# Weight sums', sample and state transfers issued by GpSimd, the second tokens' first gates in 256, 256 and 512 columns, and another place for the gates' buffers

## The chip, the cores and the metric

One core of a Trainium2 chip runs the kernel. The metric is the device time of one execution in microseconds; the time before is the median of three runs. A profile of one execution stands beside it. Its engines are called PE (TensorE), DVE (VectorE), ACT (ScalarE), POOL (GpSimd) and SP (SyncE, which only issues transfers here). SPq, ACTq and POOLq are the queues in which SP, ACT and POOL issue DMAs, each in its own order.

## The reference

One layer of a hybrid decoder: 2048 prompt tokens of width 1024 in one batch, and 8 sample sequences of one token each with states of their own.

```python
ada = silu(c) @ w_ada + b_ada
shift, scale, gate = split(ada, 3)
hn = rmsnorm(x, g_norm) * (1 + scale) + shift
z = hn @ w_in                                  # 1024 -> 5136
xa, za, q, k, v, glr, zg = split(z, ...)       # 1024, 1024, 512, 512, 1024, 16, 1024

xc = conv_b + sum(xp[:, j:j + T] * conv_w[j] for j in range(4))
gx = sigmoid(blocks(xc) @ w_gate_x + b_gate_x)     # 8 blocks of 128
ga = sigmoid(blocks(xc) @ w_gate_a + b_gate_a)
a = exp(8 * ga * log_sigmoid(lru_lambda))
u = sqrt(1 - a * a) * gx * xc
h_t = a_t * h_{t-1} + u_t
y_lru = h * silu(za)

log_alpha = log_sigmoid(glr @ w_gla_g2 + b_gla_g2) / 16
S_t = diag(alpha_t) S_{t-1} + k_t^T v_t ; o_t = q_t S_t     # 4 heads, 128 x 256 states
y_gla = rmsnorm(o) * g_gla_norm * silu(zg)

x = x + gate * (concat(y_lru, y_gla) @ w_out)
y = rmsnorm(x, g_final)
```

The outputs are y for prompt and samples and the new states (recurrence, convolution, GLA).

## The kernel before

All products are made in split form: an operand is cut into a high part (`hh`, `hi`) and a low part (`hl`, `lo`), and each product is three matmuls, high by high, high by low and low by high. Lines 650 to 652 (`project`) make tiles of w_in's columns by tokens, with 24 matmuls for a tile; lines 335 to 337 (`value_mm`) make the GLA values; line 1515 (`product`) and line 1801 (`Pair.product`) make seven products in place of eight, from sums and differences of blocks (Strassen's scheme).

The work goes through the prompt in two halves of 1024 tokens (`TH`). In the first half, for each of the four GLA heads in the order 3, 0, 1, 2, `gla_head` makes values, keys, queries and gates and runs chunks of 128 tokens, and `lru` makes some of the eight recurrence tiles. The weights used in both halves are split once and stored in DRAM as `parts`; `weights` loads them again in the second half (line 302: `w<-parts`) into one of three buffers with tag `w`.

Between the halves, `lru_last_a` normalizes and modulates the second tokens (`modulate`: PE transposes, ACT scales, POOL writes `hh` at line 201, DVE writes `hl` at line 202). These steps lie in a list, `drips`, of which `project` runs one after every second block of 128 rows. Then come `gates_ahead` (the gates of head 3, by `project`), and `gates_seven` and `lru_seven` for the three other heads and two recurrence tiles, with seven products. ACT stores the gates to DRAM (`zgd`, lines 1576 and 1603), and `gate_load` (line 1174) brings them back when a head of the second half needs them. In the second half `gla_head(1, h)` and `lru` alternate; the last stage, from line 1645, multiplies by w_out, with seven products for each pair of token tiles, from sums of w_out's blocks (`wd`, `wd2`).

Those sums are made beside the other work. `pair_weights` loads a pair of w_in's column tiles (`tr`, line 749), makes four differences with DVE, splits them and stores them (`twd`, line 763), five pairs in all. When it is done, `out_weights` starts: 16 steps, each of which loads a part of w_out (`r`, line 810), multiplies it by the gate, makes the sums (line 828), in half of the steps splits two of them (lines 832 and 833), and stores seven or nine pieces (lines 837 and 846). It stops ahead of the second tokens' preparation and goes on in the second half.

The order of this side work is written by a clock of units: `after(units, f)` puts a function off, and `tick` moves the clock on, by one unit for each projected tile and by half a unit for each value tile, and runs what is due. `behind(V)` queues what it encloses behind the last DVE instruction. `tc.tile_pool` gives buffers by tag; a buffer of a tag, or a pool opened where another was closed, waits for the last use of what lay there. A list scheduler with costs of its own puts independent instructions into each engine's order; within an engine they run in that order, so that what stands behind a waiting instruction waits too.

The pool `sp`, opened by `open_sp`, holds the buffers of the second tokens' preparation in six places of equal size with tags s0 to s5, in order of allocation: `fs4` (s0, s1, s2), `xst` (s3, s4, s5), and later over them the operands of the seven products and, at tag s2, `zq`, the buffers of the last gates. `close_sp` closes it and opens the pools of the second half's heads, whose values `vh` and `vl` are the first to be written.

Of the kernel before, what the change touches and what calls it, by code (L numbers as in the profile page):

```python
# [54 lines left out]
def hybrid_kernel(ctx, tc, i, o):  # L55
# [588 lines left out]
    def project(w, c0, n, mid=None):  # L644
# [3 lines left out]
        for kt in range(KT):  # L648
# [6 lines left out]
            if kt % 2:  # L655
                drip()
# [84 lines left out]
    def pair_weights(n=0):  # L741
# [6 lines left out]
        for a, col in enumerate(cols[n]):  # L748
            SP.dma_start(r[:, a], i["w_in"][0, :, col:col + P].rearrange("(k p) n -> p k n", p=P))
# [5 lines left out]
        def split(k, x):  # L755
            def f():
# [3 lines left out]

                def store():
                    for u, y in enumerate((t.bitcast(F32), x)):
                        SP.dma_start(twd[n, k, :, u], y.rearrange("p k n -> p (k n)"))

                after(0.5, store)
            return f

        def one(ops):
            if not ops:
                pair_weights(n + 1)  # L770
                return
            with behind(V):
                for f in ops[0]:
                    f()
            after(0.5, lambda: one(ops[1:]))

        halves = [split(k, x) for k, x in enumerate((b11, b22, b12, b21))]
        after(1.5, lambda: one([[sub(b11, b12, b11), sub(b12, b22, b12)], [sub(b22, b22, b11), sub(b21, b21, b22)],
                                halves[:2], halves[2:]]))

    def out_weights(s0=0):


        def begin(s):
# [5 lines left out]
            SP.dma_start(g, dram(gated, (8 + 32 * q) * 256, [[0, P], [64 * 256, 2], [1, 256]]))  # L790
            SP.dma_start(bt, dram(i["b_ada"], 2 * D + q * 256, [[0, P], [512, 2], [1, 256]]))
# [13 lines left out]
        def load(s):  # L805
            q, f, m = where(s)
            r = hp.tile([P, 2, 2, 256], F32, tag="r", name="r")
            for a in range(2):
                k = CTS[f] + 4 * a + m
                SP.dma_start(r[:, a], i["w_out"][0, k * P:(k + 1) * P].rearrange("p (b n) -> p b n", b=2)[:, :, q * 256:q * 256 + 256])  # L810
            return r

        def one(ops, end):
# [5 lines left out]
            after(0.5, (lambda: one(ops[1:], end)) if ops[1:] else end)  # L819

        def step(s, r, g):
# [8 lines left out]
            def split(n, x):  # L830
# [3 lines left out]

                def store2():
                    for h in range(2):
                        SP.dma_start(wd2[n, :, h, m, c], p[:, h].bitcast(F32))

                after(0.5, store2)

            def store():

                for x, ops in ((r[:, 0], (B11, T1)), (r[:, 1], (B21, B22)), (t, (T2, T3, T4))):
                    for n, k in enumerate(ops):
                        if not (f and k in (B22, T4)):
                            SP.dma_start(wd[f, k, :, m, c], x[:, n])
                if outw["stop"] or s == 15:
                    outw["busy"], outw["next"] = False, s + 1
                elif s % 8 < 7:
                    after(0.5, lambda: again(s + 1, g))  # L850
                elif q == 0:
                    after(0.5, lambda: begin(s + 1))
# [4 lines left out]
                + ([[lambda: split(0, b22), lambda: split(1, t[:, 2])]] if f else []), lambda: after(0.5, store))  # L857

        def again(s, g):
            r = load(s)  # L860
            after(1.5, lambda: step(s, r, g))
# [1352 lines left out]
```

## Time and profile before

| | us |
|---|---|
| median of 3 runs | 1481.87 |
| lowest and highest | 1480.29, 1484.11 |
| the profiled execution | 1483.09 |
| its span | 1481.3 |
| PE busy | 1432.7 |
| DVE busy | 1050.7 |
| ACT busy | 691.2 |
| POOL busy | 30.0 |

The span is the time from the first to the last instruction in the profile. Busy time of PE is not PE at its peak: matmuls overlap, and a matmul after idle time can run at a lower clock. In the lists of waits, a row names the waiting engine, tile and line, then what it waited for, then total, number and longest. In a timeline a row has the start, the duration, the engine, the line, the operation with its tiles, and in brackets the idle time before it and what ended it.

### The profile page before, as it was taken

To read this page: it belongs to the slowest core of one execution; us is meant where nothing else is said; L and a number is where in the kernel's file an instruction comes from. 1 tells how busy PE (TensorE), PEld (TensorE's weight loads), DVE (VectorE), ACT (ScalarE), POOL (GpSimd) and SP (SyncE) were. 2 spreads that over 40 slices of the span, in tenths; PEclk is the share of its full clock that TensorE was granted. 3 is DMA by queue.
4 is the path that set the end of the run, shared out by engine and by line. 5 is a ranking of instruction groups with operands and counts; after the bars stand their busy time and mean duration, and the time that the engine had idled before them with its cause. 6 is when DMAs were issued, how large, how long until landed. Compare 5 with 4: busy or idle time off the path is not lost.

```text
span 1481.3 us, 23382 instructions
## 1 busy us (share of the span) xinstructions
PE 1432.7 (97%) x8693; PEld 1253.9 (85%) x8693; DVE 1050.7 (71%) x2471; ACT 691.2 (47%) x1253; POOL 30.0 (2%) x44
## 2 busy tenths in 40 slices
PE   8999999999999999999899999798999999999998
PEld 6888989889898887787799999798998887778886
DVE  5757667765765868844458688487678886588886
ACT  4654544652554466633354444445457622244342
POOL 0200000000000002000000000000000000000000
PEclk9999999999999999999999999899999999999999
DMA  9656976856555554666836647467462757793453
GB/s 328 256 181 206 302 261 204 262 164 201 176 188 189 177 189 147 220 217 220 302 116 203 225 148 225 137 205 240 143 209 91 298 179 270 262 354 120 141 174 114
DMA packets 206135, 305.31 MB, mean 206 GB/s; under 512 B 13570, under 2 KB 143778, under 8 KB 203581
## 3 DMA queue, kind: packets, MB, share of 16 engines
q1 hardware_dynamic: 171317, 282.58, 56.9%
q10 hardware_dynamic: 34352, 20.19, 4.4%
q8 instruction: 68, 1.11, 0.3%
q0 software_dynamic: 352, 1.05, 0.2%
q14 instruction: 46, 0.38, 0.1%
HBM read 188.51 MB, written 115.33 MB: 205 GB/s over the span
## 4 chain that ended last, share of the span: by engine, by line
PE 77%; DVE 11%; DMA 6%; ACT 4%; issue 2%; SPq 0%; POOL 0%; ACTq 0%; DVEq 0%
PE acc L1801 12%; PE acc L650 10%; PE acc L651 10%; PE acc L652 10%; PE tp L1801 9%; PE acc L1515 5%; PE acc L335 3%; PE acc L336 3%; PE acc L337 3%; DMA w<-parts 3%; PE po L1045 1%; DVE cv L1239 1%; PE tp L1131 1%; DMA tr<-in_w_in_dram 1%; PE acc L1276 1%
## 5 line engine op out<-in xcount | busy, mean ns | idle before, releaser
L650 PE MATMUL acc<-hh,w 128*128 128x512 f32 (+3 forms) x1096 | 385.4, 352 | 14.4 <-DMA w<-parts 14.1
L651 PE MATMUL acc<-hl,w 128*128 128x512 f32 (+3 forms) x1096 | 374.4, 342 | 2.7 <-DVE hl L202 2.7
L652 PE MATMUL acc<-hh,w 128*128 128x512 f32 (+3 forms) x1096 | 373.9, 341 | 0.0
L650 PEld LDWEIGHTS acc<-hh,w 128*128 128x128 f32 x1096 | 207.6, 189 | 34.2 <-issue 10.0
L651 PEld LDWEIGHTS acc<-hl,w 128*128 128x128 f32 x1096 | 207.6, 189 | 20.9 <-DVE hl L202 4.2
L652 PEld LDWEIGHTS acc<-hh,w 128*128 128x128 f32 x1096 | 207.3, 189 | 17.0
L1801 PE MATMUL acc<-w,a 128*128 128x512 f32 (+1 forms) x792 | 184.8, 386 | 0.0
L1801 PEld LDWEIGHTS acc<-w,a 128*128 128x128 f32 x792 | 146.8, 188 | 33.2 <-issue 3.4
L335 PE MATMUL acc<-w,hh 128*128 128x256 f32 (+1 forms) x508 | 145.8, 287 | 2.4 <-DVE zq L1098 1.3
L337 PE MATMUL acc<-w,hl 128*128 128x256 f32 (+1 forms) x508 | 143.4, 282 | 0.0
L336 PE MATMUL acc<-w,hh 128*128 128x256 f32 (+1 forms) x508 | 143.3, 282 | 0.0
L1801 PE MATMUL tp<-w,a 128*128 128x512 f32 x564 | 136.0, 391 | 0.0
L1801 PEld LDWEIGHTS tp<-w,a 128*128 128x128 f32 x564 | 105.3, 188 | 26.8 <-issue 5.2
L335 PEld LDWEIGHTS acc<-w,hh 128*128 128x128 f32 x508 | 96.4, 190 | 5.2 <-DVE zq L1098 1.8
L337 PEld LDWEIGHTS acc<-w,hl 128*128 128x128 f32 x508 | 96.7, 190 | 0.0
L336 PEld LDWEIGHTS acc<-w,hh 128*128 128x128 f32 x508 | 96.4, 190 | 0.1
L1097 ACT ACTIVATE zs<-acc 128x512 f32<-128x512 f32 (+3 forms) x69 | 34.4, 498 | 104.9 <-PE acc L652 97.6
L1239 DVE SCALAR_TENSOR_TENSOR cv<-xa,vecT,cv 128x512 f32<-128x512 f32 (+2 forms) x120 | 76.1, 637 | 9.2 <-ACT cv L1237 8.7
L1651 ACT CAST a<-s 128x512 fp32r<-128x512 f32 x61 | 36.5, 619 | 95.7 <-issue 36.1
L1098 DVE SCALAR_TENSOR_TENSOR zs<-zs,acc 128x512 f32<-128x512 f32 (+3 forms) x69 | 38.7, 560 | 45.6 <-ACT zs L1097 45.6
L928 ACT CAST vh<-acc 128x256 fp32r<-128x256 f32 x56 | 20.7, 371 | 89.1 <-PE acc L337 71.1
L929 DVE TENSOR_TENSOR vl<-acc,vh 128x256 fp32r<-128x256 f32 x56 | 23.5, 420 | 51.5 <-ACT vh L928 51.4
(377 smaller groups left out, 2557.3 us busy)
## 6 DMA issues: line engine op xcount, KB each, us to landing
parts<-w SPq DMA_DIRECT2D x37, 1024.0 KB
w<-parts SPq DMA_DIRECT2D x28, 1024.0 KB
wr<-in_w_in_dram SPq DMA_DIRECT2D x44, 512.0 KB
a<-mixd SPq DMA_DIRECT2D x63, 256.0 KB
w<-wd SPq DMA_DIRECT2D x12, 1024.0 KB
w<-twd SPq DMA_DIRECT2D x20, 512.0 KB
mixd<-zs ACTq DMA_DIRECT2D x34, 256.0 KB
wada<-in_w_ada_dram SPq DMA_DIRECT2D x16, 512.0 KB
```

Of the source, the lines that this page charges most:

```text
L335: PE.matmul(ps, hh[:, kt, c], hi[:, kt % 4], start=kt == 0, stop=False)
L336: PE.matmul(ps, hh[:, kt, c], lo[:, kt % 4], start=False, stop=False)
L337: PE.matmul(ps, hl[:, kt, c], hi[:, kt % 4], start=False, stop=kt == KT - 1)
L650: PE.matmul(ps[:, :n], hi[:, kt], a, start=kt == 0, stop=False)
L651: PE.matmul(ps[:, :n], hi[:, kt], b, start=False, stop=False)
L652: PE.matmul(ps[:, :n], lo[:, kt], a, start=False, stop=kt == KT - 1)
L1097: S.activation(z, ps, AF.Tanh, scale=0.5)
L1098: V.scalar_tensor_tensor(z, z, 1.0, ps, op0=OP.add, op1=OP.mult)
L1239: V.scalar_tensor_tensor(cv[:, cq], xa[:, cq.start + k:cq.stop + k], cw[k], cv[:, cq], op0=OP.mult, op1=OP.add)
L1515: PE.matmul(ps, w[:, u, k], x[v][k], start=start and (k, u, v) == (0, 0, 0), stop=(k, u) == (3, 1), skip_group_check=True)
L1651: S.copy(t[:, 0, k], (low(t) if src is None else src)[:, k])
L1801: PE.matmul(ps, t[:, u, k], w[:, v, k, c], start=(q < 3 or ps is own) and (k, u, v) == (0, 0, 0), stop=(k, u) == (3, 1), skip_group_check= ...
```

## The change

Seven things are done.

- `project` runs a drip after every second block as before when the tile is wider than 256 columns, and after every fourth block when it is not.
- GpSimd issues what SP issued before: the loads and stores of `pair_weights` and of `out_weights`, the stores of the sample values (`vsd`), and the stores of the sample GLA states.
- In `pair_weights` and `out_weights` the stores follow directly on the operations, not half a unit later, and the next load follows directly on the stores. The first operation on a loaded tile is due two units after the load, not one and a half. In `pair_weights` each operation is queued behind DVE by itself.
- In the second half, `gate_load` is called with the first chunk's products, not with the chunk's start.
- `open_sp` allocates the place s2 last, behind s3 to s5.
- `gates_ahead` makes the gates of the second tokens in pieces of 256, 256 and 512 columns, not 512 and 512.
- With that, its remaining drips are run and the sums are begun after the second piece of 256.

```diff
@@ -652,7 +652,7 @@
             PE.matmul(ps[:, :n], lo[:, kt], a, start=False, stop=kt == KT - 1)
             if mid and kt == 3:
                 mid()
-            if kt % 2:
+            if kt % 2 and (n > 256 or kt % 4 == 3):
                 drip()
         return ps[:, :n]
 
@@ -746,7 +746,7 @@
             return
         r = hp.tile([P, 2, KT, P], F32, tag="tr", name="tr")
         for a, col in enumerate(cols[n]):
-            SP.dma_start(r[:, a], i["w_in"][0, :, col:col + P].rearrange("(k p) n -> p k n", p=P))
+            G.dma_start(r[:, a], i["w_in"][0, :, col:col + P].rearrange("(k p) n -> p k n", p=P))
         b11, b21, b12, b22 = r[:, 0, :4], r[:, 0, 4:], r[:, 1, :4], r[:, 1, 4:]
 
         def sub(x, y, z):
@@ -757,25 +757,21 @@
                 t = hp.tile([P, 4, P], F32R, tag="th", name="th", bufs=2)
                 S.copy(t, x)
                 V.tensor_tensor(x, x, t.bitcast(F32), op=OP.subtract)
-
-                def store():
-                    for u, y in enumerate((t.bitcast(F32), x)):
-                        SP.dma_start(twd[n, k, :, u], y.rearrange("p k n -> p (k n)"))
-
-                after(0.5, store)
+                for u, y in enumerate((t.bitcast(F32), x)):
+                    G.dma_start(twd[n, k, :, u], y.rearrange("p k n -> p (k n)"))
             return f
 
         def one(ops):
-            if not ops:
+            for f in ops[0]:
+                with behind(V):
+                    f()
+            if ops[1:]:
+                after(0.5, lambda: one(ops[1:]))
+            else:
                 pair_weights(n + 1)
-                return
-            with behind(V):
-                for f in ops[0]:
-                    f()
-            after(0.5, lambda: one(ops[1:]))
 
         halves = [split(k, x) for k, x in enumerate((b11, b22, b12, b21))]
-        after(1.5, lambda: one([[sub(b11, b12, b11), sub(b12, b22, b12)], [sub(b22, b22, b11), sub(b21, b21, b22)],
+        after(2, lambda: one([[sub(b11, b12, b11), sub(b12, b22, b12)], [sub(b22, b22, b11), sub(b21, b21, b22)],
                                 halves[:2], halves[2:]]))
 
     def out_weights(s0=0):
@@ -787,8 +783,8 @@
 
             g = hp.tile([P, 2, 256], F32, tag="g", name="g")
             bt = hp.tile([P, 2, 256], F32, tag="t", name="bt")
-            SP.dma_start(g, dram(gated, (8 + 32 * q) * 256, [[0, P], [64 * 256, 2], [1, 256]]))
-            SP.dma_start(bt, dram(i["b_ada"], 2 * D + q * 256, [[0, P], [512, 2], [1, 256]]))
+            G.dma_start(g, dram(gated, (8 + 32 * q) * 256, [[0, P], [64 * 256, 2], [1, 256]]))
+            G.dma_start(bt, dram(i["b_ada"], 2 * D + q * 256, [[0, P], [512, 2], [1, 256]]))
             r = load(s)
 
             def add():
@@ -807,7 +803,7 @@
             r = hp.tile([P, 2, 2, 256], F32, tag="r", name="r")
             for a in range(2):
                 k = CTS[f] + 4 * a + m
-                SP.dma_start(r[:, a], i["w_out"][0, k * P:(k + 1) * P].rearrange("p (b n) -> p b n", b=2)[:, :, q * 256:q * 256 + 256])
+                G.dma_start(r[:, a], i["w_out"][0, k * P:(k + 1) * P].rearrange("p (b n) -> p b n", b=2)[:, :, q * 256:q * 256 + 256])
             return r
 
         def one(ops, end):
@@ -816,7 +812,10 @@
             with behind(V):
                 for f in ops[0]:
                     f()
-            after(0.5, (lambda: one(ops[1:], end)) if ops[1:] else end)
+            if ops[1:]:
+                after(0.5, lambda: one(ops[1:], end))
+            else:
+                end()
 
         def step(s, r, g):
             t = hp.tile([P, 3, 256], F32, tag="t", name="t")
@@ -831,34 +830,30 @@
                 p = hp.tile([P, 2, 256], F32R, tag="p", name="p", bufs=2)
                 S.copy(p[:, 0], x)
                 V.tensor_tensor(p[:, 1], x, p[:, 0].bitcast(F32), op=OP.subtract)
-
-                def store2():
-                    for h in range(2):
-                        SP.dma_start(wd2[n, :, h, m, c], p[:, h].bitcast(F32))
-
-                after(0.5, store2)
+                for h in range(2):
+                    G.dma_start(wd2[n, :, h, m, c], p[:, h].bitcast(F32))
 
             def store():
 
                 for x, ops in ((r[:, 0], (B11, T1)), (r[:, 1], (B21, B22)), (t, (T2, T3, T4))):
                     for n, k in enumerate(ops):
                         if not (f and k in (B22, T4)):
-                            SP.dma_start(wd[f, k, :, m, c], x[:, n])
+                            G.dma_start(wd[f, k, :, m, c], x[:, n])
                 if outw["stop"] or s == 15:
                     outw["busy"], outw["next"] = False, s + 1
                 elif s % 8 < 7:
-                    after(0.5, lambda: again(s + 1, g))
+                    again(s + 1, g)
                 elif q == 0:
-                    after(0.5, lambda: begin(s + 1))
+                    begin(s + 1)
 
             one([[op(r[:, 0], r[:, 0], g, OP.mult), op(r[:, 1], r[:, 1], g, OP.mult)],
                  [op(t[:, 1], b22, b12, OP.subtract), op(b12, b12, b11, OP.subtract),
                   op(t[:, 0], b22, b12, OP.subtract), op(t[:, 2], b21, t[:, 0], OP.subtract)]]
-                + ([[lambda: split(0, b22), lambda: split(1, t[:, 2])]] if f else []), lambda: after(0.5, store))
+                + ([[lambda: split(0, b22), lambda: split(1, t[:, 2])]] if f else []), store)
 
         def again(s, g):
             r = load(s)
-            after(1.5, lambda: step(s, r, g))
+            after(2, lambda: step(s, r, g))
 
         begin(s0)
 
@@ -898,7 +893,7 @@
             (S.copy if g % 2 else V.tensor_copy)(vs[r, :min(n4, DV - g * n4)], ps[r, :min(n4, DV - g * n4)])
         for g in range(4):
             c = slice(g * n4, min((g + 1) * n4, DV))
-            SP.dma_start(vsd[h][:, c], vs[32 * g:32 * g + NS, :c.stop - c.start])
+            G.dma_start(vsd[h][:, c], vs[32 * g:32 * g + NS, :c.stop - c.start])
         if n > DV:
             r = slice(96, 96 + NS)
             return low_rank(ps[r, DV - 3 * n4:n4], r, TH)
@@ -1081,7 +1076,7 @@
         po = psum.tile([P, 512], F32, tag="o", name="po", bufs=1)[:, :DV]
         for n in (3, 0, 1, 2):
             PE.matmul(po[32 * n:32 * n + 32], qm[:, b0 + n], s0[:, n], start=True, stop=True)
-        SP.dma_start(o[7][0, b0:b0 + 4, h].rearrange("b k v -> k b v"), s0)
+        G.dma_start(o[7][0, b0:b0 + 4, h].rearrange("b k v -> k b v"), s0)
         if b0 == 0:
             V.tensor_copy(os_, po)
             return
@@ -1152,10 +1147,10 @@
             nch = min(SEGS[half][s][1], TH - SEGS[half][s][0]) // P
             if c == 0:
                 prep[s, "run"] = gla_start(half, h, s, prep[s])
-                if half:
-                    gate_load(s)
                 after(PACE[half][0], lambda: chunks(s, 1), True, True)
                 return
+            if c == 1 and half:
+                gate_load(s)
             gla_chunk(half, h, s, c - 1, prep[s], prep[s, "run"], v)
             if c < nch:
                 after(PACE[half][1], lambda: chunks(s, c + 1), True, True)
@@ -1165,7 +1160,7 @@
             if s + 1 < ns:
                 after(0, lambda: chunks(s + 1, 0), True, True)
             elif half == 1:
-                SP.dma_start(o[4][0, 0, h], St[h])
+                G.dma_start(o[4][0, 0, h], St[h])
 
         def gate_load(s):
             c0, n = SEGS[half][s]
@@ -1419,8 +1414,9 @@
         hpx.close()
         nonlocal sp_
         sp_ = spx.enter_context(tc.tile_pool(name="sp", bufs=1, side="right", reuse_waits="tile"))
-        fs4[:] = [sp_.tile([P, 4, 512], F32, tag=f"s{n}", name="fs4") for n in range(3)]
+        fs4[:] = [sp_.tile([P, 4, 512], F32, tag=f"s{n}", name="fs4") for n in range(2)]
         xst[:] = [sp_.tile([P, 2, D], F32, tag=f"s{n}", name="xst") for n in range(3, 6)]
+        fs4.append(sp_.tile([P, 4, 512], F32, tag="s2", name="fs4"))
         ra[:] = [new_ra(F32) for _ in range(2)]
 
     def new_ra(dt):
@@ -1597,12 +1593,12 @@
     def gates_ahead(h):
 
         w = [weights(ZG + (2 * h + dt) * P, P) for dt in range(2)]
-        for c0, n in SEGS[0]:
+        for c0, n in ((0, 256), (256, 256), (512, 512)):
             for dt in range(2):
                 z = silu2(w[dt], c0, n)
                 S.dma_start(zgd[2 * h + dt][:, c0:c0 + n], z)
-                tick()
-            if c0 == 0:
+                tick(n / 512)
+            if c0 == 256:
                 while drips:
                     drip()
                 sums()
```

## The prediction

> **What bounds the kernel now.** I began with the page: TensorE is busy 97% of the span, so a change gains only what TensorE's idle time holds, and the clock lost behind it.
>
> ```profile
> span 1481.3 us, 23382 instructions
> ...
> PE 1432.7 (97%) x8693; PEld 1253.9 (85%) x8693; DVE 1050.7 (71%) x2471; ACT 691.2 (47%) x1253; POOL 30.0 (2%) x44
> ```
>
> That leaves 1481.3 - 1432.7 = 48.6 us idle. The waits of TensorE (line, what was waited for: total us, times, longest) say which part of it this change can reach, and the waits of SP's queue say what SP stood behind.
>
> ```profile
> PE acc L650 <- DMA w<-parts: 14.1, 3, 8.0
> PE tp L878 <- DVE g L872: 3.0, 1, 3.0
> PE acc L651 <- DVE hl L202: 2.7, 2, 2.5
> ...
> SPq L846 <- DVE r L828: 80.7, 19, 20.2
> SPq L837 <- DVE p L833: 27.4, 6, 6.9
> ```
>
> Three kinds carry 19.8 us: stored weight parts that land late in the second half's heads (14.1), one transpose in the first of those heads (3.0), and the first gate of the second tokens (2.7). SP meanwhile stood 108 us for VectorE with stores of weight sums at its head (L846, L837), and it issues in order: the weight parts are queued behind.
>
> **The change part by part.**
>
> *The gates in 256, 256, 512 columns.* What do narrower matmuls cost? The PE timeline in the same view, 512 and 256 columns:
>
> ```profile
> 565.41 0.39 PE L650 MATMUL acc<-hh,w 128*128 128x512 f32 x1
> 565.64 0.39 PE L651 MATMUL acc<-hl,w 128*128 128x512 f32 x1
> ...
> 818.78 0.28 PE L337 MATMUL acc<-w,hl 128*128 128x256 f32 x1
> 818.89 0.28 PE L335 MATMUL acc<-w,hh 128*128 128x256 f32 x1
> ```
>
> Starts lie 0.23 us apart at 512 columns and 0.11 us at 256: the pace goes with the columns, and 96 matmuls of 256 (10.9 us) replace 48 of 512 (10.9 us) at no cost on TensorE. Two more SiLU pairs and two more stores fall on ScalarE and VectorE; I put 0.5 us against it.
>
> What it removes is in the next rows (DVE's timeline, then PE's):
>
> ```profile
> 571.61 2.90 DVE L202 TENSOR_TENSOR hl<-fs,hh 128x512 fp32r<-128x512 f32 x4
> ...
> 576.25 0.68 DVE L202 TENSOR_TENSOR hl<-fs,hh 128x512 fp32r<-128x512 f32 x1
> ...
> 576.98 0.50 PE L651 MATMUL acc<-hl,w 128*128 128x512 f32 x1 [2.50 <-DVE hl L202]
> ...
> 578.01 0.63 PE L651 MATMUL acc<-hl,w 128*128 128x512 f32 x1
> 578.44 0.63 PE L652 MATMUL acc<-hh,w 128*128 128x512 f32 x1
> ```
>
> The four low parts of the first 256 tokens are complete at 574.5, when PE comes to the gate. The old first gate reads 512 columns, so it stands for the first low part of the next 256 tokens, written at 576.25 to 576.93. The new first gates read finished columns alone: two tiles of 24 matmuls, 5.4 us of work, lie over the gap. Behind the stall the starts are 0.43 us apart where 0.23 is the pace; seven such starts cost 1.4 us more. So 2.7 + 1.4 = 4.1 us; the next 256 tokens' last low parts can still be late, so I take 3.5 (bounds 2.0 and 4.1).
>
> *The gates' buffers elsewhere.* These are ScalarE's and PE's timelines at the start of the second half:
>
> ```profile
> 728.92 0.37 ACT L928 CAST vh<-acc 128x256 fp32r<-128x256 f32 x1 [8.23 <-DMA zgd<-zq]
> ...
> 730.41 0.16 PE L878 MATMUL tp<-ident,g 8*48 8x8 f32 x1 [3.01 <-DVE g L872]
> ...
> 731.71 0.43 PE L335 MATMUL acc<-w,hh 128*128 128x272 f32 x1
> 731.93 0.43 PE L336 MATMUL acc<-w,hh 128*128 128x272 f32 x1
> ```
>
> The values' first high part may not be written until the gates' last store has landed, because it lies where the gates' buffers lay. ScalarE stands 8.23 us, VectorE and then PE behind it. With tag s2 allocated last, that place goes to an operand that PE read earlier; what lies at the new place is written later than 728.9, or I would be wrong. The 3.0 us go, and with them the slow starts (0.22 us where 0.12 is the pace, some 16 of them, 1.6 us): 4.6 at most, of which I take 4.5 (lower bound 3.0).
>
> *Transfers on GpSimd.* It takes over 240 issues: 10 loads and 40 stores of pair sums, 6 of gates and biases, 32 loads and 128 stores of output-weight sums, 16 of sample values, 8 of sample states. GpSimd's own price shows in its six present issues:
>
> ```profile
> L664 POOL DMA_DIRECT2D mixd<-zs x6 | 4.7, 777 | 551.3 <-DVE zs L1313 551.3
> ...
> mixd<-zs POOLq DMA_DIRECT2D x4, 192.0 KB, 5.6
> ```
>
> At 0.78 us the 240 take 187 us of an engine that is busy 30 of 1481; only the 16 modulating copies lie on PE's path, and the weight sums pause there, so I cost GpSimd's time at nothing. What covers it is that every load is issued two units ahead of its use; one unit is a tile of 24 matmuls, 5.4 us.
>
> What SP gains is seen at the third head (SP's queue, then PE, then the landing in the chain of waits):
>
> ```profile
> 926.63 2.17 SPq L846 DMA_DIRECT2D wd<-r  x3
> 928.86 0.44 SPq L1174 DMA_DIRECT2D zs<-zgd  x1
> ...
> 930.36 0.92 SPq L846 DMA_DIRECT2D wd<-t  x2
> 932.66 1.22 SPq L810 DMA_DIRECT2D r<-in_w_out_dram  x2
> 933.92 1.26 SPq L302 DMA_DIRECT2D w<-parts  x2
> ...
> 929.25 0.28 PE L337 MATMUL acc<-w,hl 128*128 128x256 f32 x1
> ...
> 933.53 0.34 PE L652 MATMUL acc<-hh,w 128*128 128x384 f32 x1
> 941.91 0.66 PE L650 MATMUL acc<-hh,w 128*128 128x384 f32 x1 [8.04 <-DMA w<-parts]
> ...
> 942.69 0.52 PE L652 MATMUL acc<-hh,w 128*128 128x384 f32 x1
> 943.01 0.52 PE L650 MATMUL acc<-hh,w 128*128 128x384 f32 x1
> ...
> 933.92 7.86 DMA w<-parts
> ```
>
> PE has read the values' weights by 929.25 and wants the query weights at 933.7. They are issued at 933.92 and take 7.86 us. Without L846 and L810 ahead SP would be done with the gates' loads at 929.3: landing 937.2, a stall of 3.5 instead of 8.0. The gates' loads themselves move a unit later, from the chunk's start to its first product, and may fall behind the query weights; the buffer's first half is free about 1.4 us before 929.25, so 927.9 + 6.9 (the shorter landing below) leaves 1.1. I take 2.5: a gain of 5.5, and 1.0 of the 1.9 us of slow starts (0.32 us where 0.17 is the pace, some 13 of them): 6.5, bounds 4.5 and 8.9.
>
> The two other heads:
>
> ```profile
> 1029.69 1.59 SPq L837 DMA_DIRECT2D wd<-p  x3
> 1031.38 0.54 SPq L302 DMA_DIRECT2D w<-parts  x1
> ...
> 1037.44 0.41 PE L650 MATMUL acc<-hh,w 128*128 128x384 f32 x1 [3.59 <-DMA w<-parts]
> ...
> 837.55 6.94 DMA w<-parts
> ...
> 844.63 0.41 PE L650 MATMUL acc<-hh,w 128*128 128x384 f32 x1 [2.48 <-DMA w<-parts]
> ```
>
> In the fourth head the stores put the issue off to 1031.38. I take 3.0 for it (bounds 0 and 5.1, the stall and its slow starts). In the second the issue at 837.55 came when PE had only just let go of the buffer, so little is to be had: 0.6 (0 to 2.5).
>
> The sum: 3.5 + 4.5 + 6.5 + 3.0 + 0.6 = 18.1, less 0.5 for the narrow gates and 0.6 for what is late next in the heads: 17 us off. The profiled execution took 1483.1 (1481.3 in its span), 1.2 above the median of 1481.9, so 1466 by the profile, 1465 by the median. All lower bounds together give 9.5 - 1.1 = 8.4 off (1473), all upper ones 25 off (1457).
>
> The sums' steps also run quicker: without the waits of half a unit before each store and each next load, a step lasts 2.5 units, or 3 with a split, not 3.5 or 4. More of the 16 steps then fit in the first half, where PE is full and VectorE is not, and the second half's heads get VectorE time back. I count nothing for it.
>
> **The rivals.**
>
> *Landing, not issue, is the limit.* The parts cannot start before PE frees a buffer, and GpSimd's transfers now run beside them rather than queued before them. Speaking for it is the second head: issued at once, 6.94 us to land, 2.48 idle. Speaking against is 929.3 before 933.92. Then the three heads keep about 10 of their 14.1 us; the gain is 3.5 + 4.5 + 4 - 1 = 11, or about 1471. The Trainium skill's page DMA: Bandwidth & Descriptors ("Issuing engines are not separate DMA queues") says just this, that all issuers share 16 engines and only the sequencer's issue time is saved; the 5 us between 928.86 and 933.92 are such issue time, so trace and rule agree there.
>
> *The stalls move.* PE comes earlier to the next late thing and loses as much there: about 1480, no measurable change. VectorE is busy 71% overall; nothing shows a second wait of such a size right behind each of these.
>
> *The turnaround on GpSimd makes VectorE stand (slower).* A sums buffer is stored, must land, is loaded again, and VectorE's next step is due two units (10.9 us) on; VectorE works in order, so a late load stops the evictions that PE's banks wait for. The chain of waits before has the longest turnaround so far:
>
> ```profile
> 172.95 5.20 DMA twd<-tr
> 178.65 8.82 DMA tr<-in_w_in_dram
> ```
>
> That is 14.0 us, 3.1 over the 10.9; VectorE's idle 29% of a 10.9 us span absorbs 3.2. So it decides from about 14 us, and every microsecond beyond costs 21 us over 5 pair and 16 output steps; 1.2 us beyond gives 1465 + 25 = 1490. Against it: the other turnaround in that chain was short, and output steps load a quarter of the bytes. The Trainium skill's page SBUF — State Buffer ("Who interferes with whom") speaks for it: VectorE's faster two-port modes lock GpSimd out of writing descriptors for a whole instruction. No run here yet shows that; before, GpSimd issued only six transfers, all late.
>
> **How the numbers follow.** The forecast has 0.60, landing as the limit 0.20, moved stalls 0.08, the slow turnaround 0.12. A measurement of this kernel can tell about 0.3% (4.4 us) from no change. Faster is then 0.80, same 0.08, slower 0.12. The range runs from 1456, just under the sum of the upper bounds, to 1482, which takes in the moved stalls and leaves out the slow case and little else.
>
> **What would show it.** Right: no DMA wait over 4 us at the heads' L650, no ACT wait on zgd at L928, no hl wait over 1 us at the first gate, SP's queue without VectorE waits at its stores, POOL busy near 200 us, the clock's dips there gone. Wrong: VectorE waiting on r or tr loads, or PE on VectorE evictions in the first half; w<-parts waits as long as before in spite of earlier issues; a new ScalarE or VectorE wait on zgd.

## The result, and the profile after

The changed kernel took 1496.12 us (median of 4, 1494.74 to 1501.72) beside 1481.78 of the kernel before: a ratio of 1.0102, 95% interval 1.0073 to 1.0132. It is 1.0% slower, where 1465 was forecast. The profiled execution took 1495.5, 1493.7 of it in the span, 12.4 more than before.

From the head of the page after:

```profile
span 1493.7 us, 23572 instructions
PE 1437.0 (96%) x8741; PEld 1259.8 (84%) x8741; DVE 1052.3 (70%) x2473; ACT 690.7 (46%) x1255; POOL 175.1 (12%) x288
```

The page's numbers look harmless. TensorE is busy 4 us more and waits 8 us more; GpSimd's 244 more instructions (the 240 transfers counted, and four stores of the prompt's own GLA states) cost it 145 us, less than the 187 counted. The waits of PE after, then of VectorE, name the trouble (line, what was waited for: total us, times, longest):

```profile
PE tp L1006 <- DVE xb L991: 10.0, 3, 4.1
PE tp L1126 <- DVE on L1053: 6.4, 1, 6.4
PE acc L335 <- DVE vl L924: 4.0, 1, 4.0
...
PE tp L197 <- ACT ra L200: 2.4, 1, 2.4
...
PE acc L650 <- DMA w<-parts: 0.7, 1, 0.7
```

```profile
DVE r L827 <- DMA r<-in_w_out_dram: 17.6, 6, 4.8
DVE tr L753 <- DMA tr<-in_w_in_dram: 14.3, 3, 6.2
...
DVE tr L753 <- issue: 6.6, 1, 6.6
```

(The last row is a fourth wait at the first operation on a loaded pair; the view doesn't name the load there.) PE's wait for stored weight parts at L650 is nearly gone, 14.1 to 0.7. In its place PE waits for VectorE's evictions, and VectorE for the loads of sums that GpSimd issues. To see where that falls I laid the same matmuls of both PE timelines beside one another and took the later kernel's start less the earlier's, at the end of each stage. Each number is the delay so far in us (negative: ahead of the kernel before); the kernels e2 to e15 are explained below.

```
                     pair sums  1st half  gates  2nd half  2nd head  3rd head  4th head   span
kernel                     320       500    720       735       860       960      1080   less 1481.3
changed                   23.6      29.1   27.5      22.4      27.4      17.9      12.2     12.4
e8  one wide load         16.8      21.8   20.4      15.2      19.4       8.9       3.8      5.0
e11 loads split           15.5      21.7   22.2      16.9      21.4      10.9       5.6      7.6
e2  pair loads on SP       1.8       7.8    6.3       1.8       6.1      -4.4      -9.6     -8.0
e5  pair sums on SP       -0.1      -1.3   -0.7      -4.9      -1.4     -11.4     -16.7    -15.1
e9  slow sums, SP          0.2       0.1    0.8      -3.4       0.9       1.2       0.9      1.7
e14 quick sums, SP        -0.8      -1.9   -3.9      -8.5       3.8      -6.2      -9.0     -8.1
e15 slow sums, GpSimd     -0.7      -0.7   -2.0      -6.1      -6.4     -10.2      -9.8     -7.2
```

(Below the names of the stages are the times in the kernel before at which they end.) In the changed kernel 23.6 us go while the pair sums run and 5.5 behind them; from there 16.9 come back. So 29 us are lost where the prediction had put nothing. The 16.9 are close to its sum of 17, but not made of its parts, as the section on why it was wrong shows.

How 4 us are lost, in order, from the timelines of GpSimd, VectorE and PE:

```profile
149.09 1.08 POOL L761 DMA_DIRECT2D twd<-tr  x2 [0.92 <-DVE tr L759]
154.27 0.92 POOL L749 DMA_DIRECT2D tr<-in_w_in_dram  x1 [4.10 <-DMA twd<-tr]
160.80 0.90 POOL L749 DMA_DIRECT2D tr<-in_w_in_dram  x1 [5.61 <-issue]
...
168.23 0.69 DVE L753 TENSOR_TENSOR tr<-tr 128x512 f32<-128x512 f32 x1 [5.87 <-DMA tr<-in_w_in_dram]
...
169.86 0.42 DVE L924 TENSOR_TENSOR vl<-acc,vh 128x256 fp32r<-128x256 f32 x1
...
170.33 0.58 PE L335 MATMUL acc<-w,hh 128*128 128x256 f32 x1 [3.98 <-DVE vl L924]
```

GpSimd waits for the last store to land, writes the first load of the pair in 0.92 us, stands 5.61 us for nothing that the timeline names, and writes the second. That one has landed by 168.23, 18.6 us after the last store was issued (149.09 + 0.54); VectorE came to it at 162.4, stood, and with it the low part of the values that is queued behind on VectorE and for which PE's bank waits. The next pairs stand 4.09, 3.98 and 4.00 us in the same place. The view of transfers tells what ends the stand (KB, then us from issue to landing of the pair's first load):

```profile
tr<-in_w_in_dram POOLq DMA_DIRECT2D x1, 512.0 KB, 6.1
```

Issued at 154.27, the first load landed at 160.4; the second was written from 160.80. In all five pairs the second is written 0.3 to 0.4 us after the first has landed.

The 5.5 us behind the pair sums are lost in the same way, at a load of output-weight sums (VectorE, then PE). In e5, explained below, VectorE has no such wait there, and PE has none either.

```profile
464.45 0.69 DVE L827 TENSOR_TENSOR r<-r,g 128x512 f32<-128x512 f32 x1 [4.84 <-DMA r<-in_w_out_dram]
...
480.17 0.58 PE L1006 MATMUL tp<-xb,e 128*128 128x128 f32 x1 [4.11 <-DVE xb L991]
```

### The profile page after: what moved, and what is told of

It reads as the page before. It is cut to its first block, busy times and chain, and to the rows that moved or that the text cites. A ratio compares the mean times of both kernels' runs of the same rounds, so it can differ in the third digit from the quotient of the medians.

```text
span 1493.7 us, 23572 instructions
## 1 busy us (share of the span) xinstructions
PE 1437.0 (96%) x8741; PEld 1259.8 (84%) x8741; DVE 1052.3 (70%) x2473; ACT 690.7 (46%) x1255; POOL 175.1 (12%) x288
## 4 chain that ended last, share of the span: by engine, by line
PE 53%; DVE 5%; ACT 4%; DMA 3%; issue 2%; POOL 1%; ACTq 0%; POOLq 0%; DVEq 0%
PE acc L1797 12%; PE tp L1797 8%; PE acc L1511 6%; PE acc L650 5%; PE acc L652 5%; PE acc L651 5%; PE acc L335 1%; PE acc L337 1%; PE acc L336 1%; DMA w<-parts 1%; PE po L1040 1%; PE tp L1006 1%; DVE cv L1234 1%; ACT L945 1%; DMA wd<-r 1%
## 5 line engine op out<-in xcount | busy, mean ns | idle before, releaser
L650 PE MATMUL acc<-hh,w 128*128 128x512 f32 (+3 forms) x1112 | 388.5, 350 | 3.3 <-POOL hh L201 1.5
L650 PEld LDWEIGHTS acc<-hh,w 128*128 128x128 f32 x1112 | 211.2, 190 | 23.2 <-POOL hh L201 2.4
L651 PEld LDWEIGHTS acc<-hl,w 128*128 128x128 f32 x1112 | 211.4, 190 | 16.5 <-DVE hl L202 0.2
L652 PEld LDWEIGHTS acc<-hh,w 128*128 128x128 f32 x1112 | 210.8, 190 | 17.0 <-DVE w L300 0.6
```

Source lines behind the costliest of these rows:

```text
L650: PE.matmul(ps[:, :n], hi[:, kt], a, start=kt == 0, stop=False)
L651: PE.matmul(ps[:, :n], hi[:, kt], b, start=False, stop=False)
L652: PE.matmul(ps[:, :n], lo[:, kt], a, start=False, stop=kt == KT - 1)
```

## Experiments on the first half

**Which sums?** My theory: the turnaround (store, landing, load, landing) is longer on GpSimd than the two units of cover. Rival: GpSimd's issues slow VectorE itself. Three kernels, and one with the other parts of the change alone.

*e1, the pair sums due later, all else as changed.*

```
-        after(2, lambda: one([[sub(b11, b12, b11), ...     # pair_weights
+        after(3.5, lambda: one([[sub(b11, b12, b11), ...
```

> The changed kernel with one number changed: the first VectorE operation on a loaded pair of column tiles is due 3.5 units after the load, not 2. All transfers stay on GpSimd. Theory, turnaround: TensorE lost 24 us in the first half (6.9, 1.5, 9.2 and 6.3 us near 165, 190, 235 and 265 us) because VectorE, in its own order, stood 21 us for tr loads that come back some 19 us after the last store and are due after 11. With 19 us of allowance the stands go: VectorE's waits on tr under 3 us, and 1496 - 22 = 1474 us. Rival, ports: GpSimd's writing of descriptors holds VectorE up wherever it happens; then nothing changes, 1496. Rival, cadence: the quicker sums simply put VectorE's work at worse places; then pairs that come later move the loss, 1485 to 1500.

*e2, only the pair loads on SP.*

```
-            G.dma_start(r[:, a], i["w_in"][0, :, col:col + P]...)
+            SP.dma_start(r[:, a], i["w_in"][0, :, col:col + P]...)
```

> The changed kernel with the ten loads of pairs of column tiles issued by SP again, their stores and all else by GpSimd, due times unchanged at 2 units. Theory, space: of the 19 us of turnaround 4.0 are GpSimd standing between the first and the second load of a pair, because it may not write the second's descriptors before the first has drained. On SP the two go out 0.5 us apart, the turnaround is about 14.5, and VectorE stands some 3 us a pair: TensorE loses at most 8 of the 24 us, 1480. Rival, landing: the time lies in the landing of stores and loads whoever issues them; VectorE's waits on tr stay near 20 us and the time above 1490.

*e5, the pair sums wholly as before (SP, pauses, due after 1.5), the rest as changed.*

```
-            G.dma_start(r[:, a], i["w_in"]...), G.dma_start(twd[n, k, :, u], ...)
+            SP.dma_start(...)      # both; after(0.5, store), after(0.5, ...) to the next pair
-        after(2, lambda: one(...
+        after(1.5, lambda: one(...
```

> The changed kernel with the making of pair sums as it was before (SP issues its loads and stores, half a unit between a split and its stores and between these and the next load, 1.5 units to the first operation); output-weight sums, samples, states, gates and place as changed. Theory, turnaround: the 24 us of the first half go and the 5.1 us near 460 and the second head's 4.7 stay: 1472 to 1474. Rival, ports: 190 of the 240 transfers are still on GpSimd, so most of the loss stays: above 1488.

Measured: e1 1480.4 us (ratio to the kernel before 0.9981, 0.9966 to 0.9997), e2 1473.1 (0.9934, 0.9911 to 0.9957), e5 1466.9 (0.9886, 0.9864 to 0.9908). With more cover the first half loses 4.1 us in place of 29; with the loads on SP 7.8, of which 6.0 are output sums; with the pair sums on SP nothing. So the 23.6 us are the pair sums' loads on GpSimd. e1 missed its 1474 by 6 us: in its trace the last two pairs still wait 3.8 and 4.7 us for tr (the stand lasts up to 7.6 us there), and 7.2 us are lost in the second head. e2 and e5 did better than expected. e5 lands near the 1465 forecast, because its output sums, still on GpSimd with two units of cover, lose nothing in the first half: those 5.5 us aren't a fixed price, but depend on where the steps fall. Nor is VectorE itself slower: its 20 operations at L753 take 684 ns in the middle both before and after. And GpSimd isn't held either: the 56 stores of one kind took 542 to 587 ns (row below, in the section on the heads), so none was held for the length of a VectorE instruction (0.69 us above). The Trainium skill's page SBUF — State Buffer ("Who interferes with whom"), which I had cited for this rival, names a lock that no run here shows.

**Why does GpSimd stand between two loads?** Theory: the descriptors of one load's 1024 runs leave no space for 1024 more until they have gone. Rival: it is the bytes and their landing.

*e8, one load of 1 KB runs where a pair's two columns are neighbours (the first three pairs; the last two keep two loads).*

```
-        r = hp.tile([P, 2, KT, P], F32, tag="tr", name="tr")
+        r = hp.tile([P, KT, 2, P], F32, tag="tr", name="tr")
+        if cols[n][1] == cols[n][0] + P:
+            G.dma_start(r.rearrange("p k a n -> p k (a n)"), ...2 * P columns...)
+        else: ...two loads, as before...
```

> The changed kernel, all its transfers on GpSimd, but the two 128-column loads of a pair sum are one load of 256 columns where the two columns are neighbours (the first three pairs): half as many runs, each 1 KB instead of 512 bytes. The last two pairs keep two loads. Theory: GpSimd stands some 4 us before the second load of a pair because the descriptors of 1024 runs leave no space for 1024 more. With one load that gap is gone in the first three pairs, the load lands some 4 to 5 us earlier, VectorE's waits for tr there fall from 5.9, 2.3 and 6.2 us to below 2 each, and the first half loses about 12 us less: 1482 to 1485. Rival: the time lies in the landing of the stores and of the bytes; then the waits stay as they are and the time is 1494 to 1496.

*e11, each load in two halves, 512 runs each.*

```
-            G.dma_start(r[:, a], ...1024 rows...)
+            for k in (0, 4):
+                G.dma_start(r[:, a, k:k + 4], ...512 rows...)
```

> The changed kernel with each of the two loads of a pair (1024 runs of 512 bytes) issued as two loads of 512 runs; same bytes, same runs, same order. If GpSimd stands 4 us between the two loads because its ring has no space for more runs until earlier ones have gone, the first two of the four are issued back to back and the stands of the others add up to about the same 4 us: time within 3 us of the changed kernel's 1496. Rival: each load stands for the one ahead of it, whatever its size: three stands of about 4 us each, landing some 8 us later and the first half losing some 25 us more: 1520.

e8 took 1490.6 us (1.0056, 1.0035 to 1.0077), e11 1487.2 (1.0041, 1.0022 to 1.0060). GpSimd's timeline, first e8 (one wide load, then a pair of two), then e11 (the halves):

```profile
178.89 0.91 POOL L749 DMA_DIRECT2D tr<-in_w_in_dram  x1 [3.73 <-DMA twd<-tr]
...
215.44 0.90 POOL L753 DMA_DIRECT2D tr<-in_w_in_dram  x1 [8.18 <-DMA twd<-tr]
220.29 0.90 POOL L753 DMA_DIRECT2D tr<-in_w_in_dram  x1 [3.96 <-issue]
```

```profile
154.35 2.26 POOL L750 DMA_DIRECT2D tr<-in_w_in_dram  x3 [4.20 <-DMA twd<-tr]
159.60 0.75 POOL L750 DMA_DIRECT2D tr<-in_w_in_dram  x1 [2.99 <-issue]
```

One wide load of the same bytes, 1024 runs of 1 KB, is written in 0.91 us and no stand follows. In e8 the first wide pair costs PE nothing where it had cost 6.7 us, the second 1.6 as before, and the two pairs that kept two loads lose 9.2 and 6.6, as in the changed kernel (9.2 and 6.7). In e11 three halves, 1536 runs, go back to back, and the fourth stands 2.99, again until the first of them has landed (159.24; it is written from 159.60). So it is neither the bytes nor the number of loads, but the count of runs not yet landed: 1536 fit, 2048 don't. Where between them the limit lies, and what holds the descriptors, was not measured. e8 gained less than the 12 us expected, because the third of the waits that I had counted, 6.2 us, belongs to a pair that kept two loads. e11 gained 9 us where I expected about the same time: since 1536 runs start at once and not 1024, the last part starts sooner.

**Is cover enough for all on GpSimd?** *e6: the pair sums due after 3.5 units, the output sums after 3, every transfer on GpSimd.*

```
-        after(2, lambda: one(...          # pair_weights
+        after(3.5, lambda: one(...
-            after(2, lambda: step(s, r, g))    # out_weights
+            after(3, lambda: step(s, r, g))
```

> The changed kernel, every transfer on GpSimd as changed, with nothing altered but two due times: the pair sums' first operation 3.5 units after its load instead of 2, the output sums' 3 instead of 2. Theory: GpSimd's transfers cost only where their cover is too short, so the rest of the first half's loss goes too (the waits for r that the kernel with later pair sums alone still had: 10.8 us in four, at 1480 us): about 1470. Rival: beyond the turnaround GpSimd's issues cost something themselves (VectorE or the copies behind them); then it stays at 1480.

It took 1479.8 us (0.9980, 0.9963 to 0.9996): the rival's number, though not for its reason. The first half is as in e1 (5.2 lost), but the sums, a unit longer each, now last until 992 us, and the third head waits for its weight parts again. That leads to the heads.

## Experiments on the heads

e5 came near the sum of the prediction. Was it for the reason given, SP's queue? *e9 puts the output-weight sums back on SP with their pauses, and keeps the rest of e5.*

```
-            G.dma_start(g, ...), G.dma_start(bt, ...), G.dma_start(r[:, a], ...), G.dma_start(wd2[n, ...), G.dma_start(wd[f, ...)
+            SP.dma_start(...)        # all five, and after(0.5, ...) ahead of each store and next load, due after 1.5
```

> The changed kernel with the pair sums and all loads and stores of the output-weight sums on SP as before, with their pauses; the sample values and sample states still go by GpSimd, the gates' loads are still issued a unit later, and the gates and their buffers are as changed. Theory: what freed SP in the second half's heads is the stores and loads of weight sums that stood ahead of the weight parts; with them back on SP the third and fourth head lose again what they lost before (waits of about 8 and 3.6 us for w<-parts), some 12 to 14 us more than with the sums on GpSimd: about 1479. Rival: the later gates' loads and the sample stores did it; then the heads stay quick and the time is about 1466.

It took 1483.3 us (1.0010, 0.9995 to 1.0025): all of the gain is gone, with waits of 7.8 and 4.1 us for w<-parts in the third and fourth head. But e9 takes back two things, and the view of one line's instructions shows the second: how long the sums run. Their stores (durations in ns: least, median, most; then the first and the last start), in the kernel before and after:

```profile
L846 SPq DMA_DIRECT2D wd<-r x56: 319/354/1221, 308.2 to 1064.8; - x56
```

```profile
L841 POOL DMA_DIRECT2D wd<-r x56: 542/560/587, 316.3 to 874.7; - x56
```

Without the pauses the sums are done before the third head begins; the prediction had seen that a step gets shorter and counted "nothing for it". So two kernels more, the other corners of the square, each with the rest of e5: *e14, sums on SP in the quick order; e15, sums on GpSimd in the slow order.*

```
e14:  e5 with G.dma_start -> SP.dma_start in out_weights
e15:  e9 with SP.dma_start -> G.dma_start in out_weights
```

> The kernel with pair sums on SP, its output-weight sums on SP too, but in the changed kernel's quick order (no pause of half a unit before a store or the next load, due two units after the load). Two things were changed at once for these sums, the engine that issues and the pace: before, they run until 1065.7 us, in the changed kernel until 875 us, ahead of the third head. If it is the pace (sums gone before the third and fourth head come to their weight parts), those heads' waits for w<-parts stay away: near 1467, or 1470 if SP's standing for VectorE costs something in the first half. If it is the engine, SP stands at the stores and the third head loses its 8 us or more again: 1480 or slower.

> The other half of the same pair: the output-weight sums on GpSimd, but in the old slow order (all pauses of half a unit back, due one and a half units after the load); they will last to about 1060 us again. If the pace is what saved the third and fourth head, both lose again what the slow sums on SP lost (waits of 8 and 3.6 us): about 1480. If SP's freedom is what counts (my prediction: the weight parts are no longer queued behind stores), the third head's wait falls to about 3.5 us and the fourth's to less than 1: 1468 to 1472.

```
                     slow order (to 1053-1066 us)        quick order (to 875-890 us)
sums on SP           e9   1483.3 (1.0010, .9995-1.0025) e14  1475.9 (0.9962, .9946-.9977)
sums on GpSimd       e15  1474.4 (0.9944, .9924-.9964)    e5   1466.9 (0.9886, .9864-.9908)
```

By the medians each of the two is worth 7 to 9 us (by the ratios to the kernel before 7 to 11), and they add up: neither theory holds alone. The rows say how. The third head in e15 (SP's queue, the landing in the chain of waits, PE):

```profile
922.89 1.89 SPq L302 DMA_DIRECT2D w<-parts  x2
...
922.89 9.21 DMA w<-parts
...
932.24 0.66 PE L650 MATMUL acc<-hh,w 128*128 128x384 f32 x1 [3.67 <-DMA w<-parts]
```

and in the changed kernel (SP, then PE at the keys and at the queries, the last two from PE's timeline and the chain):

```profile
955.24 1.89 SPq L302 DMA_DIRECT2D w<-parts  x2
...
956.59 0.34 PE L650 MATMUL acc<-hh,w 128*128 128x384 f32 x1
...
961.72 0.41 PE acc L650
```

In both SP issues the query weights 1.3 us before PE begins the keys, where in the kernel before it issued them 4.7 after PE's last read for the values. That is what a free SP gives: 8.0 us of stall become 3.7. In e15 the query weights take 9.21 us to land, with 0.56 MB of GpSimd's transfers beside them; in the changed kernel, with no sums left, they have landed by 961.72, in 6.5 us or less, and the stall is gone. e6 shows it again: sums to 992, the landing 9.05, the stall 4.13. And e14 shows what the engine is for: its sums are still running in the second head, and there the old stall appears, SP issuing the parts at 838.81 behind nine stores and two loads of sums:

```profile
846.49 0.66 PE L650 MATMUL acc<-hh,w 128*128 128x384 f32 x1 [8.05 <-DMA w<-parts]
```

It loses 12 us in that head (table, -8.5 to 3.8) and gains 10 in the third. e15's third head gains 3.8; nearly 5 us are lost behind it (a wait of 3.9 for ScalarE's vs, which I did not follow up), the fourth gains 4.5, and it ends 7.2 ahead.

*Did the other moved transfers matter? e13: as e5, but sample values and states by SP and the gates' loads at their old place. e7 and e12: e5 and e13 with the output sums due after 3 units, against what VectorE still waits for r.*

```
e13:  G.dma_start -> SP.dma_start for vsd, o[7], o[4]; gate_load(s) back at c == 0
e7, e12:  -            after(2, lambda: step(s, r, g))
          +            after(3, lambda: step(s, r, g))
```

> The kernel with pair sums on SP, and of the other moved transfers only the output-weight sums and their gates on GpSimd: the sample values and sample states go by SP as before, the gates' loads stand at their old place ahead of the chunk. The counterpart of the kernel in which only those were moved (1483, where the buffers' place alone should have made it 1480 or less). Theory: the sums are all of the gain: 1463 to 1467. Rival: SP needs both cleared ahead of the weight parts, and the gates' loads and sample stores bring part of the third head's wait back (up to 5 us by the prediction's count of SP's issue time): about 1471.

> The changed kernel with the pair sums as before (SP, with their pauses), and the output-weight sums' first operation due three units after their loads instead of two. If the turnaround on GpSimd is what is left of the loss (a load issued behind its landing stores arrives after VectorE comes to it), the one unit more takes the waits of VectorE for r loads away (7.1 us in four waits with two units, 5.8 of them ahead of the second head) and with them some 5 us of the second head: about 1462. Rival: the late loads only show where PE is short of evictions anyway, and a step that lasts a unit longer pushes sums into the later heads: 1467, no difference from the kernel with two units.

> As the kernel with only the output sums on GpSimd, its sums due three units after their loads instead of two. The unit more took VectorE's waits for r from 7.1 to 3.9 us once and 1.5 us of the time, within what the runs can tell: 1462 to 1466 here if the sums are all of the gain, 1470 if the sample transfers on GpSimd were part of it.

e13 took 1471.8 us (0.9924, 0.9904 to 0.9943), e12 1468.1 (0.9904, 0.9880 to 0.9929), e7 1465.3 (0.9886, 0.9863 to 0.9910). So the gain is mostly the sums'; the rest of the moved transfers is worth 3 to 5 us by the medians, at the edge of what the intervals tell. In the traces 2.3 us of e13's are lost where the second half starts, and not for want of a free SP: without the sample values' stores ahead of them in GpSimd's queue, the sums' next loads go out from 700.91 to 705.85 (in e5 the first of them only at 725.57), and PE then waits 3.4 us for the values' weight parts, 1.4 in e5. e12 has the same (3.7). The later due time did not bring the 5 us that I expected: e7 has e5's ratio. VectorE no longer waits for r before the second head, but that head still costs 2.5 us there (3.5 in e5), now with a wait of 2.9 for VectorE's e: r was not what held it.

## Experiments on the gates and their buffers

*e4: the kernel before with the narrow gates and the buffers' place alone. e10: e5 with the gates in 512, 512 again.*

```
-        for c0, n in SEGS[0]:                                   # e4 (e10 the reverse)
+        for c0, n in ((0, 256), (256, 256), (512, 512)):
-        fs4[:] = [... for n in range(3)]                        # e4
+        fs4[:] = [... for n in range(2)]
+        fs4.append(sp_.tile([P, 4, 512], F32, tag="s2", name="fs4"))
```

> The kernel before with two parts of the change alone: the gates in 256, 256 and 512 columns, and place s2 allocated last. In the changed kernel TensorE drew in 1.5 us at the gates and 5.1 at the start of the second half. Theory: both belong to these parts and not to GpSimd: 1481.8 - 6.5 = 1475. Rival: without GpSimd's transfers SP's sample stores hold up the start of the second half and only 2 to 3 us come: 1479.

> The changed kernel with the pair sums as before on SP, and the second tokens' first gates in 512, 512 columns again. My prediction gave the narrow gates 3.5 us, less 0.5: by that this kernel takes about 1470 where the one with narrow gates takes 1467. What the traces of the changed kernels show (the wait for the low parts gone, a wait for the modulating chain of 2 to 3 us in its place) says 0 to 1.5 us: 1467 to 1468.

e4 took 1481.7 us (0.9982, 0.9968 to 0.9995), 7 us more than the theory's 1475; e10 took 1469.8 (0.9919, 0.9896 to 0.9941). The place does what was said: in every kernel of the table above 4 to 5 us are won where the second half starts (between the columns 720 and 735), and 4.8 in e4, which has no transfer moved. e13 keeps 2.1 of it and e12 none, for the reason just told. No kernel has the place alone; that the gain is the place's is read from this stage. ScalarE's first copy there, which had stood 8.23 us for a store of the gates, waits in the changed kernel only for PE's product:

```profile
751.46 0.37 ACT L923 CAST vh<-acc 128x256 fp32r<-128x256 f32 x1 [3.24 <-PE acc L337]
```

In e4 half of it goes again: PE comes to the second head sooner, its weights no sooner (a wait of 2.99 for w<-parts, 2.48 before), and 2.5 of the 4.8 us are lost there. The narrow gates are worth little by the traces. In e10 (PE's timeline) the stall that they should remove is back, and another is ahead of it:

```profile
568.23 0.66 PE L197 MATMUL tp<-ident,xt 128*128 128x128 f32 x4 [2.11 <-ACT fs L200]
...
580.43 0.50 PE L651 MATMUL acc<-hl,w 128*128 128x512 f32 x1 [1.18 <-DVE hl L202]
```

The first row stands in e5 alike (2.12): PE gets there and waits for the chain that modulates the tokens, not for one low part. Side by side, e5 gains 1.3 us on e10 at the gates; in e4, where they are narrow and no transfer is moved, that stage takes 0.9 us longer than before. The medians of e5 and e10 lie 2.9 us apart, which would fit the prediction's 3.0, but their intervals overlap and can't decide it.

## Why the prediction was wrong

- **The step that failed** is "I cost GpSimd's time at nothing. What covers it is that every load is issued two units ahead of its use". The writing was priced well (0.92 us for a pair load, 0.54 to 0.56 for a store). The time from the last store to the load's landing wasn't: it was 18.6 us in the pair above, 5.6 of it a stand that no row of before contains, against 10.9 of cover. It cost 23.6 us in the four pair steps that follow one another, about 6 a step, and 5.5 in the output sums. That the rest comes to 16.9 where 17 was forecast is luck: gates, place, third, fourth and second head gave 1.6, 5.1, 9.5, 5.7 and -5.0, where 3.5, 4.5, 6.5, 3.0 and 0.6 were predicted (less 1.1).
- **The rival named for it** had the mechanism, the queue behind VectorE. That it also had nearly the time (1490, measured 1496) is luck: it put 1.2 us on each of 21 steps, and the loss was about 6 on each of four and 5.5 behind them. Its bound was wrong by my choice of row: I took SP's longest turnaround, 14.0 us, as GpSimd's, and gave it a chance of 0.12.
- **The gates**: 3.5 predicted (2.0 to 4.1), 1.6 in the changed kernel's trace and 1.3 between e10 and e5. The wait of 2.5 us for hl went, and PE waited for ScalarE instead (2.4 at L197 in the changed kernel). A stall that ends at an engine which is itself late is not worth its length.
- **The buffers' place**: 4.5 predicted, 4.8 in e4, 5.1 in the changed kernel. What is late next, 0.6 predicted, was 2.5 in e4.
- **The third and fourth head**: 6.5 and 3.0 predicted, 9.5 and 5.7 measured. The engine was half the reason. Its size came out (a stall of 3.5 predicted, 3.67 in e15), but by two errors that cancel: SP issued 1.3 us before the keys where 0.2 was reckoned (929.3 against 929.54), and landing took 9.21 us, not 7.86. The other half is the step counted at nothing, the quicker order, which ends the sums before these heads. The rival that landing is the limit was right about the half that remained in e15. The Trainium skill's page DMA: Bandwidth & Descriptors ("Issuing engines are not separate DMA queues") says that only issue time is saved: the trace agrees for that half, 4.7 us after against 1.3 before.
- **The second head**: 0.6 won was predicted, 5.0 were lost. The timelines after point to the same failed step, VectorE waiting for a load of sums and PE then for VectorE; but e7, where VectorE doesn't wait for r there, still loses 2.5, so only a part of it can be that step's. The rest stays open.

```profile
866.86 0.69 DVE L827 TENSOR_TENSOR r<-r,g 128x512 f32<-128x512 f32 x1 [4.23 <-DMA r<-in_w_out_dram]
...
875.52 0.73 PE L1006 MATMUL tp<-xb,e 128*128 128x128 f32 x3 [3.45 <-DVE xb L991]
```

The version that beats both is e5, or e7: the pair sums left on SP, the rest changed; 1.1% faster than the kernel before.

## What to carry to other kernels

Moving a transfer to another queue moves its whole turnaround there: add up the wait for landing, the issue, any stand between issues, and the landing, and compare it with the cover, load by load; an in-order engine that waits for it stops everything queued behind. When a change alters both who issues and when, run the two apart before giving either the credit. Price a removed stall by what is late right behind it.

## What the runs showed of the hardware

GpSimd's price for a transfer grows little with its runs (contiguous pieces), then jumps. From GpSimd's groups after (count | busy us, mean ns | idle before and its releasers):

```profile
L841 POOL DMA_DIRECT2D wd<-t x40 | 21.7, 544 | 62.1 <-DVE t L827 42.0 <-DVE r L827 14.3 <-DVE S L1041 3.4
L806 POOL DMA_DIRECT2D r<-in_w_out_dram x32 | 23.1, 726 | 10.6 <-DMA wd<-r 7.9 <-issue 2.5
L749 POOL DMA_DIRECT2D tr<-in_w_in_dram x10 | 9.2, 924 | 50.5 <-issue 23.8 <-DMA twd<-tr 20.2 <-DVE rs_t L151 6.5
```

128 runs take 0.54 us, 256 take 0.73, 512 take 0.75 (e11) and 1024 take 0.92; but 2048 in a row add a stand until the first 1024 have landed, 4 to 6 us each and 23.8 over five pairs, which is booked as idle and not as busy. Runs of 1 KB cost GpSimd what runs of 512 bytes do. And a transfer of stored weight parts of 1 MB, with a second right behind it, had landed in 6.5 us or less when no sums ran, in 7.9 behind SP's sums, and in 9.1 to 9.2 with 0.6 to 0.9 MB of GpSimd's transfers beside it.
